# Value projections by seven block products, the convolution's norm by halves beside them, key copies spread over the steps

## The chip, the cores and the metric

The kernel is one program on one core of a Trainium2 chip. The metric is the device time of one execution in microseconds (us). The median of three runs before the change is 1679.09 us. A core has a matrix engine (TensorE, PE in the profile), a vector engine (VectorE, DVE), a scalar engine (ScalarE, ACT), GpSimd (POOL) and SyncE (SP), whose queue issues nearly all transfers here. Each engine works through its own list of instructions in order and waits on semaphores for the others.

## The reference

One block on 1024 tokens with 1024 channels, float32 throughout:

```
h = rms_norm(x, g_pre_mix)
z = h @ w_in            # q, k, v (3 groups x 8 heads x 64 each), glu_in (2048), z_ga, z_gc (1024 each)
y_attn = dilated_attention_mixer(q, k, v)          # groups (window, dilation): (128,1) (512,4) (2048,16)
y_conv = conformer_conv_mixer(glu_in)              # GLU, depthwise conv of 31 taps, layer_norm, silu, @ w_conv_out
merged = sigmoid(z_ga) * y_attn + sigmoid(z_gc) * y_conv
x = x + rms_norm(merged @ w_mix_out, g_post_mix)
x = x + rms_norm(swiglu_ffn(rms_norm(x, g_pre_ffn), w_ffn_in, w_ffn_out), g_post_ffn)
```

Within the attention each of the three groups gives an output and a log of its softmax denominator for each head; the three outputs of a head slot are added with the softmax of these logs as weights, and the sum (512 wide) goes through `w_attn_out`. The layer norm of the convolution is taken over the channels, for each token.

## The kernel before, in words

**Products.** Every float32 operand is split into two fp32r parts, `hi` (a rounded copy, ScalarE, L214) and `lo` (what is left, a subtraction on POOL or VectorE, L215); a product is hi·hi + hi·lo + lo·hi, three matmuls. Most projections are written by `winograd`: two weights' blocks and two token halves with seven block products in place of eight, from sums of weight blocks (`quarters`) and sums of token blocks T1 to T4 (`quarter_sums`). The six value jobs (`v`, two halves of the heads for each of three groups) are plain instead. For each of 8 tiles of 128 tokens and each of 8 channel blocks there is one matmul over 512 columns (L1137, the tokens' hi against the weights' hi and lo side by side) and one over 256 (L1138, the tokens' lo against the weights' hi). ScalarE copies the bank and POOL adds its two halves (L1159).

**The stages.** With channels on partitions, the gates, the convolution's input and the queries and keys are projected first (span 0 to 543.7 us), while VectorE works on the depthwise convolution. Then come the six value jobs, one late gate (`plain_gate`), sixteen convolution-out units (`unit`, L336 to L338, each 8 blocks x 3 matmuls over 512 tokens, closed on VectorE by L1947), sixteen attention-out units of half the length, the mix projection (L2025) and the feed-forward layers (L352 to L354, L2281).

**What runs beside them.** Order is set by counting. Each `tick` of a product hands on background work: steps put off with `later(k, ...)` run k ticks on, and generators given to `bg` go on after as many ticks as they yield. `conv_norm`, the layer norm of the convolution, is such a generator: it starts with the means over channels (L1499, two matmuls with a column of 1/1024 against `csum`, which the end of the convolution fills), then subtracts, squares, sums, takes the reciprocal root (`rstd`) and applies gain and silu, over 1024 tokens at a time. Eight blocks of the convolution come back from memory for it.

The attention is a generator too, moved on by `beat`: each call adds `RATE` to a credit and each whole credit is one small step (RV = 0.42 beside value products, RU = 0.8 beside units). It has 12 stacks (3 groups x 4 pairs of heads) of 8 steps u, so 96 steps, in a pipeline: `att_s` the scores (L1258, L1262), `att_e` the exponentials, `att_t` transposes (L1301, copies L1308 and L1309), `att_p` the products with the values (L1335), `att_o` the outputs. A stack needs its keys twice, with the other head's rows zeroed; `double` makes that tile on POOL (L1076 to L1078), for both heads at once, at u == 7 of the stack before and at u == 2 of its own. `stack_load` fetches queries, keys and values.

**The merge.** For each of the four head pairs `merge` waits until the attention has ended, and then multiplies, adds and splits the three groups' outputs on VectorE: L1438, L1442, L1447, L1452 (each 128 x 1024), L1457 (a sum with a change of order), a copy on ScalarE (L214) and L215. The results are the operands `OT` of the attention-out units; the block kt of such a unit needs the merge of pair kt. What a merge has not yet issued when the convolution-out units are over is issued there in one go (`B.finish`).

**Loads around the units.** The second convolution-out weights are loaded 14 ticks into the late gate, the first gate tile (`d_gc`) 1 tick after it. The first three units take the first token half of three output blocks, the next three the second; after that the halves alternate.

Of the kernel before, what the change touches and what calls it, by code (L numbers as in the profile page):

```python
# [15 lines left out]
T = 1024  # L16
D = 1024
KT = 8
H = 512
# [29 lines left out]
NSLOT = 42  # L49

# [14 lines left out]
class Build:  # L65
# [236 lines left out]
    def pair(self, i):  # L302
# [12 lines left out]
        if n < len(J) and J[n][2] == "row1":  # L315
# [5 lines left out]
            self.queued = n + 2  # L321
        elif n < len(J):
            todo += [(3, lambda: self.load_ahead(n + 1)), (16, lambda: self.queue_split(n + 1))]
# [139 lines left out]
    def rstd(self, acc, n, eps_col, gap=3):  # L463
# [3 lines left out]
        ps = self.bank("s")  # L467
# [13 lines left out]
        for b in range(0, nt, 4):  # L481
            pb = self.bank("s")
# [587 lines left out]
    def double(self, p, hf):  # L1070
# [3 lines left out]
        z = ops["z"][hf] = self.slot(F32R)  # L1074
        for h in range(2):
# [88 lines left out]

    LT, LP = 4, 5
# [4 lines left out]
    def attention(self):  # L1170
# [12 lines left out]
        while s < total + self.LP:  # L1183
            if s < total:
# [33 lines left out]
                for _ in range(1 + (u == 1 and not order)):  # L1218
                    if nxt and nxt[5] < 5:
                        self.stack_load(nxt)  # L1220
# [263 lines left out]
    def conv_norm(self):  # L1484
        nc = self.nc
        mean = self.slot()
        A = []

        def load():
            A.append(self.slot())  # L1490
            nc.sync.dma_start(A[-1], self.d_conv[len(A) - 1])

        for _ in range(4):
            load()
        yield 3
        for hf in range(2):
            s = slice(hf * H, (hf + 1) * H)
            ps = self.bank("s")
            nc.tensor.matmul(ps, self.mean_col.to_broadcast([128, 128]), self.csum[:, s], start=True, stop=True)  # L1499
            nc.scalar.copy(mean[:, s], ps)  # L1500
        self.csum = None
        yield 1
        q = []
        for b in range(10):
            if b < 4:
                load()
            if b < 8:
                nc.vector.tensor_tensor(A[b], A[b], mean, op=OP.subtract)
            if 0 < b < 9:
                q.append(self.slot())  # L1510
                nc.scalar.activation(q[-1], A[b - 1], AF.Square)
            if b > 2:
                p = q.pop(0)
                nc.vector.tensor_tensor(q[0], q[0], p, op=OP.add)
            p = None
            yield 3 - b % 2
        mean = None
        yield 3
        pb = yield from self.rstd(q[0], T, self.eps_ln, 6)
        rs = self.slot()  # L1520
        for hf in range(2):
# [875 lines left out]
```

## Time and profile before

| what | value |
|---|---|
| runs | 1680.42, 1679.09, 1678.84 us (median 1679.09) |
| profiled execution, its own time | 1681.52 us |
| its span | 1679.7 us |
| TensorE busy | 1661.0 us (99%), 8027 matmuls |
| VectorE, ScalarE, POOL busy | 1272.0, 828.0, 543.2 us |
| mean granted TensorE clock | 0.998 |
| transfers | 289.64 MB, mean 172 GB/s |
| value jobs end, convolution-out units end (span) | 771.6, 905.8 us |

"Span" is the time from the first to the last recorded instruction; the execution's own time is a little longer. The busy time of an engine is the sum of its instructions' durations, and a group's row gives busy time, mean ns of one, idle time before it and what ended that idleness. A line number (L1137) is the line of the kernel that issued the instruction. PEclk and "clock" are the TensorE clock that was granted, as a share of full speed.

### The profile page before, as it was taken

How to read it: one execution, taken by the hardware profiler on the slowest of the kernel's cores; microseconds unless marked ns; L12 is line 12 of the kernel's file. 1: busy time of each engine (PE TensorE's matmuls, PEld its weight loads, DVE VectorE, ACT ScalarE, POOL GpSimd, SP SyncE). 2: the span in 40 equal slices, each digit the busy share in tenths (PEclk: the TensorE clock that was granted, in tenths of full speed). 3: DMA queues.
4: the chain of work that ended last, by engine and by line, in shares of the span. 5: the costliest groups of instructions: out<-in, count | busy, mean ns of one | idle time of the engine just before them, and what ended most of it. 6: DMA issues, size and time to landing. Idle time of an engine off the chain costs nothing.

```text
span 1679.7 us, 23382 instructions
## 1 busy us (share of the span) xinstructions
PE 1661.0 (99%) x8027; PEld 1386.2 (83%) x8027; DVE 1272.0 (76%) x2268; ACT 828.0 (49%) x1646; POOL 543.2 (32%) x456
## 2 busy tenths in 40 slices
PE   9999999999999999999899999999999999999998
PEld 7788888888888888988788888888888888888886
DVE  7998988789999767778885746877655566576686
ACT  7454443434444578888722447633333333354453
POOL 0038777887876356867300300000000000000000
PEclk9999999999999999999999999999999999999999
DMA  4435433455566887879998524134132223494334
GB/s 181 155 101 187 139 132 133 152 185 176 188 166 172 282 269 215 256 228 251 296 300 294 188 88 164 63 132 150 73 128 95 94 94 111 167 372 127 114 118 156
DMA packets 165178, 289.64 MB, mean 172 GB/s; under 512 B 47689, under 2 KB 79812, under 8 KB 165060
## 3 DMA queue, kind: packets, MB, share of 16 engines
q1 hardware_dynamic: 164420, 287.45, 52.8%
q8 instruction: 63, 1.03, 0.2%
q14 instruction: 55, 0.45, 0.1%
q10 hardware_dynamic: 288, 0.52, 0.1%
q0 software_dynamic: 352, 0.18, 0.1%
HBM read 197.39 MB, written 95.42 MB: 174 GB/s over the span
## 4 chain that ended last, share of the span: by engine, by line
PE 85%; issue 5%; POOL 3%; DMA 3%; DVE 2%; ACT 2%; SPq 0%; DVEq 0%; POOLq 0%; ACTq 0%
PE p L354 16%; PE p L353 16%; PE p L352 16%; PE p L2281 12%; PE p L2025 5%; PE p L1137 4%; PE p L336 2%; PE p L337 2%; PE p L338 2%; PE p L1138 2%; PE p L655 2%; PE p L1335 1%; DMA datt<-d 1%; PE p L1301 1%; PE p L1262 1%
## 5 line engine op out<-in xcount | busy, mean ns | idle before, releaser
L352 PE MATMUL p<-b,b 128*128 128x512 f32 x1316 | 512.6, 390 | 0.0
L354 PE MATMUL p<-b,b 128*128 128x512 f32 x1316 | 512.4, 389 | 0.3
L353 PE MATMUL p<-b,b 128*128 128x512 f32 x1316 | 512.1, 389 | 0.1
L354 PEld LDWEIGHTS p<-b,b 128*128 128x128 f32 x1316 | 247.0, 188 | 52.7 <-POOL b L215 1.5
L352 PEld LDWEIGHTS p<-b,b 128*128 128x128 f32 x1316 | 247.0, 188 | 52.5 <-ACT c L411 0.5
L353 PEld LDWEIGHTS p<-b,b 128*128 128x128 f32 x1316 | 247.0, 188 | 51.7 <-DVE b L1473 0.5
L2281 PE MATMUL p<-b,b 128*128 128x512 f32 x924 | 209.6, 389 | 0.0
L2281 PEld LDWEIGHTS p<-b,b 128*128 128x128 f32 x924 | 173.4, 188 | 36.0
L868 DVE SCALAR_TENSOR_TENSOR p<-b,par,p 128x511 f32<-128x511 f32 (+14 forms) x232 | 163.5, 738 | 0.0
L1137 PE MATMUL p<-b,b 128*128 128x512 f32 x384 | 144.3, 408 | 0.1
L214 ACT CAST b<-d 128x1024 fp32r<-128x1024 f32 x82 | 86.1, 1050 | 100.6 <-POOL d L237 56.5
L215 POOL TENSOR_TENSOR b<-d,b 128x1024 fp32r<-128x1024 f32 x43 | 104.1, 2422 | 47.6 <-ACT b L214 39.0
L1473 DVE TENSOR_TENSOR b<-b,b 128x512 fp32r<-128x512 f32 x141 | 98.4, 704 | 17.9 <-ACT b L1472 16.3
L1138 PE MATMUL p<-b,b 128*128 128x256 f32 x384 | 107.9, 281 | 0.0
L215 DVE TENSOR_TENSOR b<-d,b 128x1024 fp32r<-128x1024 f32 x39 | 47.6, 1221 | 79.0 <-ACT b L214 79.0
L1472 ACT CAST b<-b 128x512 fp32r<-128x512 f32 x141 | 86.5, 619 | 41.4 <-PE p L2281 17.8
L214 ACT CAST b<-b 128x1024 fp32r<-128x1024 f32 x51 | 53.6, 1052 | 89.2 <-POOL b L246 38.8
L336 PE MATMUL p<-b,b 128*128 128x512 f32 x240 | 96.2, 401 | 0.0
L1276 ACT ACTIVATE c<-c,stat 128x128 f32<-128x128 f32 (+1 forms) x192 | 85.1, 447 | 18.8 <-DVE stat L1266 17.4
L337 PE MATMUL p<-b,b 128*128 128x512 f32 x240 | 93.6, 390 | 0.0
L338 PE MATMUL p<-b,b 128*128 128x512 f32 x240 | 93.6, 390 | 0.0
L2025 PE MATMUL p<-b,b 128*128 128x512 f32 x384 | 89.9, 392 | 0.0
(248 smaller groups left out, 2899.4 us busy)
## 6 DMA issues: line engine op xcount, KB each, us to landing
b<-w_in SPq DMA_DIRECT2D x33, 512.0 KB, 5.6
b<-w_fi SPq DMA_DIRECT2D x29, 512.0 KB, 4.3
d<-w_in SPq DMA_DIRECT2D x25, 512.0 KB, 4.5
dk<-c SPq DMA_DIRECT2D x48, 256.0 KB, 4.1
dq<-c SPq DMA_DIRECT2D x48, 256.0 KB, 3.6
b<-dk SPq DMA_DIRECT2D x48, 256.0 KB, 6.8
d<-w_fi SPq DMA_DIRECT2D x22, 512.0 KB, 3.6
dqS<-c SPq DMA_DIRECT2D x44, 256.0 KB, 2.1
```

Source lines behind the costliest of these rows:

```text
L214: self.nc.scalar.copy(hi, x)
L215: self.wsplit.tensor_tensor(lo, x, f(hi), op=OP.subtract)
L336: nc.tensor.matmul(ps, hi[:, s], a, start=kt == 0, stop=False)
L337: nc.tensor.matmul(ps, hi[:, s], b, start=False, stop=False)
L352: nc.tensor.matmul(ps, hi[:, s], a, start=first and kt == 0, stop=False, skip_group_check=True)
L353: nc.tensor.matmul(ps, hi[:, s], b, start=False, stop=False, skip_group_check=True)
L354: nc.tensor.matmul(ps, lo[:, s], a, start=False, stop=kt == 3, skip_group_check=True)
L868: nc.vector.scalar_tensor_tensor(A[i][:, j:], src[i][:, :H - j], w[i], A[i][:, j:], op0=OP.mult, op1=OP.add)
L1137: nc.tensor.matmul(ps, a, w, start=kt == 0, stop=kt == KT - 1, skip_group_check=True)
L1138: nc.tensor.matmul(ps[:, 256:], b, w[:, :256], start=False, stop=kt == KT - 1, skip_group_check=True)
L2025: nc.tensor.matmul(banks[tt][nh], st, wt[:, nh * H:(nh + 1) * H], start=bool(kt == 0 and a), stop=bool(kt == KT - 1 and b))
L2281: nc.tensor.matmul(acc[t], x, y, start=first and e == 0, stop=last and e == 2, skip_group_check=True)
```

## The change

Four of the six value jobs (`QUADS = 2`, two jobs each) leave `v` for a new function `quad`. It computes two jobs by seven block products, from sums of weight blocks (S1 to S4, A11, A12, A22) and the token sums T1 to T4 that the earlier projections used. The tokens' sums stand still as the matmul's stationary 128 x 128 operand; the weights' blocks move, 256 columns at a time. Each product is 4 channel blocks x 4 token tiles x 3 matmuls (`quad_prod`, L1216, L1218, L1219). The weights' sums are made on VectorE, their split is a copy on ScalarE and a subtraction on POOL (L1199).

The convolution's norm now works on one token half at a time and runs beside the quads; its means (L1645) are asked for when it is given to the background. The attention starts after the quads: its first loads 30 ticks into the second quad, its steps with the first of the two value jobs that are left. `double` makes one head's copies per call, at u == 6, 7, 8 and 1. The second convolution-out weights are loaded at tick 6 of the late gate, the first gate tile at tick 9 of it. Two output blocks, not three, start with their first half.

```diff
+QUADS = 2
...
     def double(self, p, hf, heads=(0, 1)):
...
-        for h in range(2):
+        for h in heads:
             nc.gpsimd.memset(f(z[parts[1 - h], h * H:(h + 1) * H]), 0.0)
             nc.gpsimd.tensor_copy(z[parts[h], h * H:(h + 1) * H], f(ops["k"][h][parts[0], s]))
             nc.gpsimd.tensor_copy(ops["c"][h][parts[1], s], f(ops["q"][parts[h], s]))
...
+    def quad_prod(self, ps, w, rhs, first):
+        hi, lo = w
+        for kt in range(4):
+            a, b = rhs[kt]
+            n = slice(kt * 256, (kt + 1) * 256)
+            for c in range(4):
+                o = ps[c // 2][:, c % 2 * 256:(c % 2 + 1) * 256]
+                t = slice(c * 128, (c + 1) * 128)
+                nc.tensor.matmul(o, a[:, t], hi[:, n], start=first and kt == 0 and c % 2 == 0, stop=False, ...)
+                nc.tensor.matmul(o, a[:, t], lo[:, n], ...)
+                nc.tensor.matmul(o, b[:, t], hi[:, n], ...)
+                if c % 2:
+                    self.tick()
...
+    def quad(self, q, T, then):
+        for k, step in ((1, lambda: self.quad_split(q, "A12")), (2, lambda: self.quad_sum(q, "S1")),
+                        (3, lambda: self.quad_sum(q, "S3")), (4, lambda: self.quad_sum(q, "S2")),
+                        (7, lambda: self.quad_sum(q, "S4")), (8, lambda: self.quad_split(q, "S2")),
+                        (13, lambda: self.quad_split(q, "S1")), (21, lambda: self.quad_split(q, "S3")),
+                        (29, lambda: self.quad_split(q, "S4")), (37, lambda: self.quad_split(q, "A22"))):
+            self.later(k, step)
...
+        X, Z = two(), two()
+        self.quad_prod(X, w.pop("A11"), operands("B11"), True)
+        x1 = copy(X, ja)
+        self.quad_prod(Z, w.pop("A12"), operands("B21"), True)
+        add(Z, x1, ja, 0)
+        self.quad_prod(X, w.pop("S2"), operands("T2"), False)
+        x2 = copy(X, ja)
+        V = two()
+        self.quad_prod(V, w.pop("S1"), operands("T1"), True)
+        v1 = copy(V, jb)
+        self.quad_prod(X, w.pop("S3"), operands("T3"), False)
+        add(X, v1, jb, 1)
+        self.quad_prod(V, w.pop("S4"), operands("B22"), False)
+        add(V, x2, ja, 1)
+        self.quad_prod(X, w.pop("A22"), operands("T4"), False)
...
-                if u == 7 and nxt:
-                    self.double(nxt, 0)
-                if u == 2:
-                    self.double(cur, 1)
+                if u in (6, 7) and nxt:
+                    self.double(nxt, 0, (u - 6,))
+                if u == 8 and nxt:
+                    self.double(nxt, 1, (0,))
+                if u == 1:
+                    self.double(cur, 1, (1,) if cur[2]["z"][1] else (0, 1))
...
     def conv_norm(self):
+        means = [average(0), average(1)]
+        self.csum = None
+        for j in range(4):
+            self.later((0, 0, 5, 10)[j] + 1, lambda j=j: load(0, j))
+        yield 5
         for hf in range(2):
...
-            B.later(14, lambda: B.load_ahead(co[1]))
+            B.later(6, lambda: B.load_ahead(co[1]))
+            B.later(9, lambda: first_gate.append(gate_load(B.d_gc[0])))
...
+    for i, q in enumerate(B.quads):
+        if i == QUADS - 1:
...
+            B.later(30, lambda: next(att))
...
+        B.quad(q, B.T, B.quads[i + 1] if i + 1 < QUADS else None)
...
+    B.fine = att
     for i, (g, hg) in enumerate(vj):
         B.v(g, hg, vs[i], vs[i + 1])
-        if i == 0:
-            next(att)
-            B.fine = att
...
-    for n, hf in [(n, hf) for hf in range(2) for n in range(3)] + [(n, hf) for n in range(3, 8) for hf in range(2)]:
+    for n, hf in [(n, hf) for hf in range(2) for n in range(2)] + [(n, hf) for n in range(2, 8) for hf in range(2)]:
```

In the rows below p is a bank of PSUM, b a tile in SBUF, d a scratch tile, c an attention tile; a tile's own number is the last one.

TensorE at the start of the value stage. Before, twenty rows of the first value job (L1137, L1138) stand ahead of the two means of the convolution's norm (L1499); these are the last four of them, the means, and what follows:

```order
L1137 MATMUL p728_4913<-b706_4800,b73_631 128x512
L1138 MATMUL p728_4913<-b706_4800,b73_631 128x256
L1137 MATMUL p728_4913<-b706_4800,b76_642 128x512
L1138 MATMUL p728_4913<-b706_4800,b76_642 128x256
L1499 MATMUL p729_4922<-b232_1635,mean_col_282 128x512
L1499 MATMUL p730_4925<-b232_1635,mean_col_282 128x512
L1137 MATMUL p728_4913<-b707_4820,b77_652 128x512
L1138 MATMUL p728_4913<-b707_4820,b77_652 128x256
```

After, six rows of the first quad's first product stand ahead of the means (L1645); these are the last three of them:

```order
L1216 MATMUL p717_4870<-b708_4818,b73_631 128x256
L1218 MATMUL p717_4870<-b709_4819,b73_631 128x256
L1219 MATMUL p717_4870<-b708_4818,b73_631 128x256
L1645 MATMUL p723_4886<-b232_1635,mean_col_282 128x512
L1645 MATMUL p725_4890<-b232_1635,mean_col_282 128x512
L1216 MATMUL p718_4871<-b708_4818,b73_631 128x256
L1218 MATMUL p718_4871<-b709_4819,b73_631 128x256
L1219 MATMUL p718_4871<-b708_4818,b73_631 128x256
```

So the means have moved from behind ten pairs of products to behind six narrow ones.

POOL where the attention starts. Before, sums of value products (L1159) stand between the key copies of the first stack's two halves (`double`, L1076 to L1078):

```order
L1077 CAST b776_5233<-b757_5111 64x512
L1078 CAST b759_5116<-b755_5106 64x512
L1159 TENSOR_TENSOR d783_5295<-b719_4879 128x512 x2
L1159 TENSOR_TENSOR d793_5405<-b719_4879 128x512 x2
L1076 MEMSET b803_5482 64x512
L1077 CAST b803_5482<-b756_5108 64x512
L1078 CAST b758_5114<-b755_5106 64x512
```

After, the last weight splits of the quads (L1199) are followed by the copies (L1083 to L1085) of both heads of the first half and then of both heads of the second, twelve rows in one piece, of which the first three are shown:

```order
L1199 TENSOR_TENSOR b807_5667<-b764_5246,b806_5666 128x1024
L1199 TENSOR_TENSOR b823_5758<-d766_5292,b822_5757 128x1024
L1083 MEMSET b826_5849 64x512
L1084 CAST b826_5849<-b810_5679 64x512
L1085 CAST b812_5685<-b809_5677 64x512
```

So no sum of value products stands any more between the copies that the first stack needs.

VectorE at the end of the merges. Before, the last row of the last merge (L215) has four ends of units (L1947) behind it, the first two of which follow here:

```order
L1947 SCALAR_TENSOR_TENSOR b1656_9289<-p1670_9375,par_306,b1656_9289 128x512
L1452 TENSOR_TENSOR d1606_8996<-d1606_8996,b1672_9385 128x1024
L1947 SCALAR_TENSOR_TENSOR b1656_9289<-p1677_9419,par_306,b1656_9289 128x512
L197 TENSOR_TENSOR b1682_9459<-b1668_9371,b1681_9458 128x512
L1457 TENSOR_TENSOR b1683_9465<-b1663_9320,d1606_8996 128x8x128
L197 TENSOR_TENSOR b1682_9459<-b1668_9371,b1681_9458 128x512
L215 TENSOR_TENSOR b1685_9479<-b1683_9465,b1684_9478 128x1024
L1947 SCALAR_TENSOR_TENSOR b1669_9373<-p1680_9451,par_306,b1669_9373 128x512
L1947 SCALAR_TENSOR_TENSOR b1669_9373<-p1686_9490,par_306,b1669_9373 128x512
```

After, the end of the last unit is the first row (L2108), and the last two rows of the third merge (L1604, L217) and the whole fourth merge (L1585 to L1604, L217) follow it, ahead of the first attention-out unit's end (L2134):

```order
L2108 SCALAR_TENSOR_TENSOR b1673_9623<-p1700_9770,par_306,b1673_9623 128x512
L1604 TENSOR_TENSOR b1702_9802<-b1676_9635,d1575_9155 128x8x128
L217 TENSOR_TENSOR b1704_9805<-b1702_9802,b1703_9804 128x1024
L1585 TENSOR_TENSOR b1697_9747<-b1697_9747,b1698_9757 128x1024
L1589 TENSOR_TENSOR b1699_9766<-b1699_9766,b1701_9778 128x1024
L1594 TENSOR_TENSOR b1697_9747<-b1697_9747,b1699_9766 128x1024
L1599 TENSOR_TENSOR d1635_9409<-d1635_9409,b1705_9809 128x1024
L1604 TENSOR_TENSOR b1706_9815<-b1697_9747,d1635_9409 128x8x128
L217 TENSOR_TENSOR b1708_9818<-b1706_9815,b1707_9817 128x1024
L199 TENSOR_TENSOR b1714_9832<-b1688_9714,b1713_9831 128x256
L2134 TENSOR_TENSOR b1689_9716<-p1712_9827,b1689_9716 128x512
```

So eight rows of merging now stand behind the end of the last unit, where none stood. In all, the attention's 96 steps stood 73 beside value products and 23 beside six units; they now stand 44 beside two value jobs and 52 beside twelve units.

More of the change, by code (lines that the diff above doesn't have):

```diff
@@ L321, in pair @@
             self.queued = n + 2
+        elif n < len(J) and J[n][2] == "values":
+            self.quad_first(self.quads[0], (2, 9, 11, 13, 19))
         elif n < len(J):
@@ L466, in rstd @@
         nt = n // 128
-        ps = self.bank("s")
+        tag = "s" if "s" in self.tags else "g"
+        ps = self.bank(tag)
         for t in range(nt):
@@ L481, in rstd @@
         for b in range(0, nt, 4):
-            pb = self.bank("s")
+            pb = self.bank(tag)
             for t in range(b, min(nt, b + 4)):
@@ new lines, in quad_prod @@
+    def quad_prod(self, ps, w, rhs, first):
+        nc = self.nc
+        hi, lo = w
[5 more added lines that the diff above has]
+                t = slice(c * 128, (c + 1) * 128)
+                nc.tensor.matmul(o, a[:, t], hi[:, n], start=first and kt == 0 and c % 2 == 0, stop=False,
+                                 skip_group_check=True)
+                nc.tensor.matmul(o, a[:, t], lo[:, n], start=False, stop=False, skip_group_check=True)
+                nc.tensor.matmul(o, b[:, t], hi[:, n], start=False, stop=kt == 3 and c % 2 == 1, skip_group_check=True)
+                if c % 2:
+                    self.tick()
@@ L1217, in attention @@
                         nxt = self.stacks(*order.pop(0))
-                for _ in range(1 + (u == 1 and not order)):
+                for _ in range(1 if order else 3):
                     if nxt and nxt[5] < 5:
@@ L1485, in conv_norm @@
         nc = self.nc
[L1486 to L1495, printed above, removed]
-        for hf in range(2):
[L1497 to L1516, printed above, removed]
@@ L1534, in conv_norm, with load, average @@
-        nc.scalar.activation(rs[:, :1], self.eps_ln, AF.Exp)
-        rs = None
-        yield 11
+        add = nc.vector.tensor_tensor
+        A = {}
+        def load(hf, j):
+            x = self.slot()
+            for e in range(2):
+                b = 2 * j + e
+                nc.sync.dma_start(x[:, e * H:(e + 1) * H], self.d_conv[b][:, hf * H:(hf + 1) * H])
+                A[hf, b] = x[:, e * H:(e + 1) * H]
+        def average(hf):
+            ps = self.bank()
+            nc.tensor.matmul(ps, self.mean_col.to_broadcast([128, 128]), self.csum[:, hf * H:(hf + 1) * H],
+                             start=True, stop=True)
+            m = self.half()
+            nc.scalar.copy(m, ps)
+            return m
@@ L1888, in build @@
     assert bl not in B.gens
-    B.banks(g=2, s=2, t=2, o=2)
-    B.bank("s")
     B.OT, B.merges = {}, []
```

180 lines of the change are left out of this document (144 added, 36 removed).

## The prediction

> **What bounds the kernel now.** I read the page first: TensorE is busy for 99% of the span.
>
> ```profile
> span 1679.7 us, 23382 instructions
> PE 1661.0 (99%) x8027; PEld 1386.2 (83%) x8027; DVE 1272.0 (76%) x2268; ACT 828.0 (49%) x1646; POOL 543.2 (32%) x456
> PE 85%; issue 5%; POOL 3%; DMA 3%; DVE 2%; ACT 2%; SPq 0%; DVEq 0%; POOLq 0%; ACTq 0%
> ```
>
> So time is won where matmul columns disappear, and lost wherever TensorE is made to wait. Next I cut the span into stages (table of windows): value jobs with the convolution's norm, value jobs with attention, attention beside the convolution-out units, those units alone, and the attention-out units. The columns are the busy times (and counts), granted clock, DMA share and GB/s.
>
> ```profile
> 543.70:612.00 68.30, 66.60 (x382) 57.37 (x382) 48.01 (x57) 44.27 (x69) 25.28 (x23) 1.00 0.87 283
> 612.00:771.60 159.60, 157.19 (x1160) 144.17 (x1161) 123.77 (x424) 133.31 (x417) 118.05 (x162) 0.99 0.82 235
> 771.60:842.00 70.40, 64.74 (x415) 54.74 (x415) 59.73 (x190) 55.23 (x172) 33.31 (x46) 1.00 1.02 283
> 842.00:905.80 63.80, 63.80 (x284) 52.69 (x283) 45.73 (x51) 14.15 (x24) 3.60 (x6) 1.00 0.93 292
> ```
>
> TensorE idles 1.7, 2.4 and 5.7 us in the first three and not at all in the fourth: that fourth stretch is 64 us of plain units, and under it VectorE finishes the attention (`merge`). Remember it; the change takes half of it away.
>
> **The products.** The start times of matmuls give their price (timeline); a record's own duration includes the pipeline.
>
> ```profile
> 560.30 0.39 PE L1137 MATMUL p<-b,b 128*128 128x512 f32 x1
> 560.53 0.28 PE L1138 MATMUL p<-b,b 128*128 128x256 f32 x1
> ...
> 574.86 0.39 PE L1137 MATMUL p<-b,b 128*128 128x512 f32 x1
> ...
> 618.23 0.39 PE L1262 MATMUL p<-b,b 128*128 128x256 f32 x2
> 618.46 0.60 PE L1301 MATMUL p<-ident,c 128*128 128x128 f32 x4
> ```
>
> A value job is 64 pairs of a 512- and a 256-wide product. From 560.30 to 574.86 there are 42 pairs: 0.347 us each. Four jobs less remove 4 x 64 x 0.347 = 88.8 us. Two `quad` calls add 2 x 7 x 48 = 672 products, all 256 wide. Two such (L1262, attention's scores), each with weights of its own, take 0.23 us to the start of the next instruction: 0.115 us each, 77.3 us in all. Gain 11.5 us. Inside a pair the 256-wide product takes 0.347 - 0.23 = 0.117 us; by that it is 78.6 us and the gain 10.2. I take the row in which narrow products follow each other, as they will in a quad: -11.5.
>
> The quads' other work lies beside them. A product of a quad lasts 48 x 0.115 = 5.5 us and needs one pair of weights, a copy on ScalarE and a subtraction on POOL:
>
> ```profile
> L214 ACT CAST b<-d 128x1024 fp32r<-128x1024 f32 x82 | 86.1, 1050 | 100.6 <-POOL d L237 56.5
> L215 POOL TENSOR_TENSOR b<-d,b 128x1024 fp32r<-128x1024 f32 x43 | 104.1, 2422 | 47.6 <-ACT b L214 39.0
> ```
>
> That is 1.05 + 2.42 us, issued at least 7 ticks (4.8 us) ahead; POOL has 7 x 2.42 = 17 us of it in the 39 us of a quad. The reads of PSUM between products have a whole other product as cover, since X, Z and V take turns. The convolution's norm keeps its operations, in halves of half the length. I cost all this at nothing; were a subtraction late at every second product, by some 0.6 us, it would be 4 us, the bound.
>
> **The norm's means, moved ahead.** As the rows of TensorE show, ten pairs of value products stood ahead of the two matmuls that sum `csum`; now six narrow ones do. What the means wait for is the end of the convolution:
>
> ```profile
> 541.30 1.08 DVE L1019 TENSOR_TENSOR c<-p,c 128x512 f32<-128x512 f32 x1
> 543.54 0.68 DVE L208 TENSOR_TENSOR b<-b,b 128x512 fp32r<-128x512 f32 x1
> 544.14 0.68 DVE L881 TENSOR_TENSOR b<-p,c 128x512 f32<-128x512 f32 x1
> 544.97 2.70 POOL L893 TENSOR_TENSOR b<-b,b 128x1024 f32<-128x1024 f32 x1 [10.32 <-DVE b L881]
> 547.73 0.70 PE L1499 MATMUL p<-b,mean_col 128*128 128x512 f32 x1 [0.25 <-POOL b L893]
> ```
>
> POOL's sum ends at 547.7. L1019 reads a product's bank in both kernels and so stays where it is; of the value weights' splits on VectorE (L208) one falls away behind it, so the sum ends some 0.6 us sooner, at 547.1. TensorE starts the stage at 543.7 and, with 0.1 us for the switch and 0.7 us of products, stands at the means at 544.5: a wait of 2.6 us where it was 0.25, so +2.4. All that is queued behind them on TensorE waits too; the other engines have work of their own and only get ahead.
>
> **The clock.** A short wait can cost more than itself (table of windows, and the waits around it):
>
> ```profile
> 609.73:613.14 3.41, 1.96 (x11) 1.43 (x10) 1.91 (x10) 3.41 (x12) 3.20 (x5) 1.00 1.05 389
> 613.14:616.56 3.42, 3.42 (x15) 3.13 (x14) 1.90 (x9) 1.82 (x7) 3.20 (x5) 0.50 1.04 215
> PE p L1258 <- POOL b L1077: 1.3, 1, 1.3
> ```
>
> After a stretch of 3.41 us with 1.96 us of work the granted clock was 0.50 for the next 3.42 us, which costs about 1.7 us. The wait for the means could do the same: +0.9 as half of it, bounds 0 and 1.7. The Trainium skill (TensorE: Matmul & The Clock Gate, "What's actually happening") says the clock halves after at least one idle window of about 3.4 us; by that rule a wait of 2.6 us would not halve it and this term would be 0. The row above disagrees, since there 1.5 us of idleness was enough.
>
> **The start of attention.** That wait of 1.3 us was for POOL. As POOL's rows show, the second pair of key copies stood behind a sum of value products (L1159), which waits for TensorE itself; now all four pairs stand together behind the last weight split of the quads, with nothing ahead of them that waits for a value job. I take the wait (1.3 us, and 0.2 us behind it) and its slow clock (1.7) as gone: -3.2, bounds 0 and -3.2.
>
> **Attention, twice as long beside the units.** Attention has 96 steps. Before, 73 stand among value products and 23 among six units; now 44 among two value jobs and 52 among twelve units. Its own matmuls are the same. The 5.7 us of idleness in 771.6 to 842 include two waits on a ScalarE or VectorE that stood for a late load:
>
> ```profile
> 802.95 0.38 PE L1335 MATMUL p<-c,b 128*128 128x256 f32 x1 [1.49 <-ACT c L1308]
> 814.16 0.44 PE L1335 MATMUL p<-c,b 128*128 128x128 f32 x2 [1.37 <-ACT c L1308]
> ACT b L196 <- DMA b<-w_co: 1.5, 1, 1.5
> DVE b L1947 <- DMA b<-dgc: 2.0, 1, 2.0
> ```
>
> The change issues both loads (the second convolution-out weights, the first gate) 8 ticks sooner: -2.9, or nothing if they are late all the same. The other 2.8 us double with the steps: +2.8. But DMA is full there (share 1.02), and a stack's keys, queries and values must come through beside twelve units now: +1.5, bounds 0 and +12.
>
> **The tail.** `merge` starts its VectorE work when attention has ended, and the attention-out units need all four merges. VectorE's rows show it: before, four units' ends follow the last merge; now the end of the third merge and all of the fourth stand behind the end of the last unit, and before the first attention-out unit. The prices (groups of VectorE and ScalarE from 841 to 893, and the first and the last row of the merges in the timeline):
>
> ```profile
> L1947 DVE SCALAR_TENSOR_TENSOR b<-p,par,b 128x512 f32<-128x512 f32 x9 | 6.7, 742 | 4.0 <-PE p L338 4.0
> L1438 DVE TENSOR_TENSOR b<-b,b 128x1024 f32<-128x1024 f32 x4 | 5.0, 1248 | 0.0
> L215 DVE TENSOR_TENSOR b<-b,b 128x1024 fp32r<-128x1024 f32 x4 | 4.9, 1232 | 0.7 <-ACT b L214 0.7
> L1447 DVE TENSOR_TENSOR b<-b,b 128x1024 f32<-128x1024 f32 x4 | 4.9, 1232 | 0.0
> L1457 DVE TENSOR_TENSOR b<-b,d 128x1024 f32<-128x1024 f32 x2 | 4.2, 2123 | 0.0
> ...
> L214 ACT CAST b<-b 128x1024 fp32r<-128x1024 f32 x4 | 4.2, 1054 | 25.4 <-DVE b L1457 25.4
> ...
> 841.98 1.23 DVE L1438 TENSOR_TENSOR b<-b,b 128x1024 f32<-128x1024 f32 x1
> ...
> 891.54 1.23 DVE L215 TENSOR_TENSOR b<-b,b 128x1024 fp32r<-128x1024 f32 x1 [0.66 <-ACT b L214]
> ```
>
> In the new order: 0.75 (the unit's end), 2.1 (L1457's successor), 1.05 on ScalarE, 1.2 for the rest of the third merge; then four times 1.2, 2.1, 1.05 on ScalarE and 1.2. That is 14.3 us, some 14.8 with the hand-overs between engines. TensorE has 9 products of the next unit that need no fourth merge, 2 us: a stall of 12.6 us. The same from the other side: the merges took from 841.98 to 892.8, 51 us; now six units are left to cover them, 6 x 24 x 0.225 = 32 us (284 products in 63.8 us), which lacks 19 us at the old pace. Bounds 10 (hand-overs cheaper, the first products longer) and 19; I take the chain, 12.6, since its ticks are dropped at the end of the units. An idle stretch of that length halves the clock again, for one window or two: +1.8, bounds 1.7 and 3.4.
>
> **The sum.** -11.5 + 2.4 + 0.9 - 3.2 - 2.9 + 2.8 + 1.5 + 12.6 + 1.8 = +4.4 us. The profiled execution took 1681.5 us (its span 1679.7), 2.4 above the median of the runs, 1679.1; on the median that is 1683.5, and I say 1684.
>
> **Rivals.** One, on the faster side: the tail is covered. If VectorE and the loads run far enough ahead that less than 6.6 us of stall is left, the time is over 0.2% below; at none, 1683.5 - 14.4 = 1669. For it: VectorE is busy 72% from 842 to 905.8, so there is room. Against it: its queue is in order and the rows stand behind the last unit's. Two: transfers starve attention beside the units. 283 GB/s at share 1.02 say that nothing is free there; 12 us more give 1695. Against: only 2.9 of 5.7 us idle were seen behind loads. Three: the narrow products are bound by their weight loads, recorded at 0.188 us each:
>
> ```profile
> L2281 PEld LDWEIGHTS p<-b,b 128*128 128x128 f32 x924 | 173.4, 188 | 36.0
> ```
>
> 672 x 0.188 = 126 us, 49 more, 1733. Against it the pair of L1262 at 0.115.
>
> **Chances.** Forecast (tail paid, 1676 to 1690) 0.62, of which 0.02 faster, 0.25 same, 0.35 slower; tail covered 0.16 (0.15 faster, 0.01 same); starved transfers 0.20; weight loads 0.02. A measurement tells 0.2%, 3.4 us, from no change. Together 0.17 faster, 0.26 same, 0.57 slower. The range 1673 to 1696 leaves out half of the second case, a fifth of the third and the fourth.
>
> **What would show it.** Right: 672 starts 0.115 us apart; L1645 waiting 2 to 3 us for POOL; no wait of attention's first steps on POOL; behind the last L2108 TensorE idle for some 8 us on ScalarE's copy of the fourth merge, with a granted clock of 0.50 after it. Wrong: TensorE without a gap between the last convolution-out unit and the first attention-out unit, or many new waits of L1482 on loads.

## The result, and the profile after

The changed kernel is slower: 1702.24 us in the median (1697.33 to 1706.53, 5 runs) against 1679.09 before, a ratio of 1.0134 with a 95% interval of 1.0118 to 1.0149. The forecast was 1684, with 1696 as its upper end: the sign was right, the size was not. The execution that was profiled took 1697.33 us (span 1695.5), 15.8 more than the one profiled before; it is the fastest of its five, so a second trace of the same kernel (a0_again, 1704.0 us, 22.5 more) is used beside it.

The page of the first trace, in its head, its chain of waits and one group:

```profile
span 1695.5 us, 23828 instructions
PE 1658.0 (98%) x8187; PEld 1391.9 (82%) x8187; DVE 1289.5 (76%) x2300; ACT 833.0 (49%) x1647; POOL 558.4 (33%) x454
PE 57%; DVE 3%; DMA 2%; ACT 1%; issue 1%; DVEq 0%; SPq 0%; ACTq 0%
L340 PE MATMUL p<-b,b 128*128 128x512 f32 x240 | 99.5, 415 | 9.2 <-ACT b L216 9.2
```

TensorE has 3.0 us less work recorded in a span that is 15.8 us longer. Where the longer time lies, the table of windows tells by stage: the quads, the two plain value jobs with attention, attention beside the units, units alone, the tail. After a stretch and its length stand the busy times (and counts) of TensorE, its weight loads, VectorE, ScalarE and POOL, then the granted clock, the DMA share and GB/s.

```profile
543.80:640.10 96.30, 89.30 (x701) 86.31 (x699) 66.96 (x83) 54.96 (x78) 45.78 (x28) 0.96 0.65 205
640.10:736.50 96.40, 92.68 (x688) 85.20 (x688) 73.48 (x251) 79.73 (x249) 67.03 (x92) 1.00 0.85 243
736.50:874.00 137.50, 130.66 (x863) 114.18 (x862) 115.51 (x378) 105.90 (x336) 75.85 (x108) 0.99 0.94 273
874.00:908.60 34.60, 34.60 (x154) 28.42 (x154) 29.89 (x37) 9.70 (x17) 2.71 (x5) 1.00 0.90 276
908.60:928.00 19.40, 9.00 (x24) 5.85 (x24) 13.83 (x12) 3.32 (x5) 1.14 (x1) 0.65 1.03 371
```

TensorE idles 7.0, 3.7, 6.8, 0 and 10.4 us in them. In the tail the forecast chain is there: the last unit ends, and VectorE (first rows) and ScalarE (last two) work through the end of the third merge and all of the fourth, while TensorE waits.

```profile
907.78 0.75 DVE L2108 SCALAR_TENSOR_TENSOR b<-p,par,b 128x512 f32<-128x512 f32 x1 [3.57 <-PE p L342]
908.44 2.01 DVE L1604 TENSOR_TENSOR b<-b,d 128x1024 f32<-128x1024 f32 x1
911.57 1.23 DVE L217 TENSOR_TENSOR b<-b,b 128x1024 fp32r<-128x1024 f32 x1 [1.11 <-ACT b L216]
...
917.50 2.00 DVE L1604 TENSOR_TENSOR b<-b,d 128x1024 f32<-128x1024 f32 x1
920.66 1.23 DVE L217 TENSOR_TENSOR b<-b,b 128x1024 fp32r<-128x1024 f32 x1 [1.17 <-ACT b L216]
910.49 1.04 ACT L216 CAST b<-b 128x1024 fp32r<-128x1024 f32 x1 [11.61 <-DVE b L1604]
919.59 1.04 ACT L216 CAST b<-b 128x1024 fp32r<-128x1024 f32 x1 [8.05 <-DVE b L1604]
```

Busy time hides part of a loss, because a record's duration includes the pipeline and a slow clock stretches it. So the table below counts lost time by the starts of the matmuls: for each, the time to the next start, less what it takes where nothing waits (0.227 us for 512 columns, 0.117 for 256, 0.058 for 128, 0.110 for a transpose), differences below zero counted as none, added up by stage. The first column goes to the attention's first score product. By these prices the change's products are 9.4 us less work. Attention beside values lasts 164 us before the change and 95 to 98 after it.

| kernel, time of the traced execution | stage's start to attention | attention beside values | attention beside units | tail |
|---|---|---|---|---|
| before, 1681.5 | 3.7 | 22.6 | 14.9 | 0 |
| changed, 1697.3 | 15.4 | 12.9 | 24.0 | 14.2 |
| changed, second trace, 1704.0 | 19.0 | 15.6 | 22.9 | 14.2 |
| e4 before, attention late, 1702.4 | 4.7 | 13.2 | 26.2 | 18.3 |
| e1 merges early, 1713.3 | 19.6 | 13.3 | 33.7 | 15.0 |
| e6 RU = 1.0, 1697.9 | 18.9 | 15.5 | 31.8 | 0.5 |
| e5 no norm arithmetic, 1689.1 | 11.5 | 10.6 | 23.1 | 14.9 |
| f1 no norm at all, 1685.9 | 7.4 | 9.9 | 24.2 | 14.0 |
| g1 splits on VectorE, 1716.6 | 25.2 | 16.8 | 24.0 | 18.1 |
| e7 one quad, 1682.2 | 7.2 | 13.4 | 16.1 | 10.1 |
| q1 one quad, RU = 0.9, 1677.9 | 8.8 | 13.5 | 18.7 | 0 |
| q2 the same, RV = 0.46, 1683.1 | 7.2 | 15.3 | 24.8 | 0 |

The sums close: the second trace loses 32.1 us more than before in the whole span (1.7 of it ahead of these stages), less 9.4 of products is 22.7, and the execution took 22.5 more.

### The profile page after: what moved, and what is told of

It reads as the page before. It is cut to its first block, busy times and chain, and to the rows that moved or that the text cites. A ratio compares the mean times of both kernels' runs of the same rounds, so it can differ in the third digit from the quotient of the medians.

```text
span 1695.5 us, 23828 instructions
## 1 busy us (share of the span) xinstructions
PE 1658.0 (98%) x8187; PEld 1391.9 (82%) x8187; DVE 1289.5 (76%) x2300; ACT 833.0 (49%) x1647; POOL 558.4 (33%) x454
## 4 chain that ended last, share of the span: by engine, by line
PE 57%; DVE 3%; DMA 2%; ACT 1%; issue 1%; DVEq 0%; SPq 0%; ACTq 0%
PE p L2442 12%; PE p L357 8%; PE p L356 8%; PE p L358 8%; PE p L2186 5%; PE p L340 2%; PE p L341 2%; PE p L342 2%; PE p L1482 2%; PE p L1144 2%; PE p L1448 1%; PE p L1409 1%; PE p L1145 1%; PE p L1405 1%; DMA b<-dq 1%
## 5 line engine op out<-in xcount | busy, mean ns | idle before, releaser
L356 PE MATMUL p<-b,b 128*128 128x512 f32 x1316 | 512.7, 390 | 0.0
L358 PE MATMUL p<-b,b 128*128 128x512 f32 x1316 | 512.4, 389 | 0.2
L357 PE MATMUL p<-b,b 128*128 128x512 f32 x1316 | 512.1, 389 | 0.1
L358 PEld LDWEIGHTS p<-b,b 128*128 128x128 f32 x1316 | 247.0, 188 | 53.2 <-POOL b L217 1.5
L356 PEld LDWEIGHTS p<-b,b 128*128 128x128 f32 x1316 | 247.0, 188 | 52.3 <-ACT c L415 0.5
L357 PEld LDWEIGHTS p<-b,b 128*128 128x128 f32 x1316 | 247.0, 188 | 51.6 <-DVE b L1620 0.5
L2442 PE MATMUL p<-b,b 128*128 128x512 f32 x924 | 209.6, 389 | 0.0
L2442 PEld LDWEIGHTS p<-b,b 128*128 128x128 f32 x924 | 173.4, 188 | 36.0
L217 POOL TENSOR_TENSOR b<-d,b 128x1024 fp32r<-128x1024 f32 x43 | 104.1, 2422 | 47.6 <-ACT b L216 39.0
L1620 DVE TENSOR_TENSOR b<-b,b 128x512 fp32r<-128x512 f32 x141 | 100.5, 719 | 15.5 <-ACT b L1619 13.8
L340 PE MATMUL p<-b,b 128*128 128x512 f32 x240 | 99.5, 415 | 9.2 <-ACT b L216 9.2
L217 DVE TENSOR_TENSOR b<-d,b 128x1024 fp32r<-128x1024 f32 x39 | 47.6, 1221 | 79.3 <-ACT b L216 79.3
L341 PE MATMUL p<-b,b 128*128 128x512 f32 x240 | 95.4, 398 | 1.2 <-DVE b L217 1.2
L342 PE MATMUL p<-b,b 128*128 128x512 f32 x240 | 95.1, 396 | 0.0
L2186 PE MATMUL p<-b,b 128*128 128x512 f32 x384 | 90.0, 392 | 0.0
L217 POOL TENSOR_TENSOR b<-b,b 128x1024 fp32r<-128x1024 f32 x24 | 57.7, 2404 | 86.6 <-ACT b L216 86.6
L2186 PEld LDWEIGHTS p<-b,b 128*128 128x128 f32 x384 | 71.4, 188 | 14.4
```

What stands on the lines that cost most here:

```text
L217: self.wsplit.tensor_tensor(lo, x, f(hi), op=OP.subtract)
L340: nc.tensor.matmul(ps, hi[:, s], a, start=kt == 0, stop=False)
L341: nc.tensor.matmul(ps, hi[:, s], b, start=False, stop=False)
L342: nc.tensor.matmul(ps, lo[:, s], a, start=False, stop=kt == nk - 1)
L356: nc.tensor.matmul(ps, hi[:, s], a, start=first and kt == 0, stop=False, skip_group_check=True)
L357: nc.tensor.matmul(ps, hi[:, s], b, start=False, stop=False, skip_group_check=True)
```

## The experiments

**The kernel again** (a0_again). No edit.

> The changed kernel once more, unaltered, as the base of the others. Its five runs lay between 1697.3 and 1706.5 us, and the profile (1697.3) is of the fastest of them. Theory: what varies are waits behind transfers, at the start of attention and beside the convolution-out units, since transfers are at full share there (1.01 to 1.04); a median of 1699 to 1705 and, in the trace, the same tail of some 14 us behind the last convolution-out unit and the same 0.120 us for a narrow product. Rival: the runs differ in the clock that follows the tail's idleness; then the tail itself differs between this trace and the first by several us.

1701.12 us (1700.53 to 1704.0). The tail is 14.2 us again. What differs most is the quads: a longer wait for the norm (L474, the reciprocal root's sums), 3.6 us where the first trace has 1.0. VectorE's wait for a load (the last row) is as long in the first trace, 5.6 us. The waits of TensorE, and that one of VectorE (us in total, times, the longest):

```profile
PE p L340 <- ACT b L216: 9.9, 2, 7.3
PE p L1482 <- DVE c L1456: 7.2, 7, 3.3
PE p L474 <- DVE c L1667: 3.6, 1, 3.6
PE p L1218 <- POOL b L1199: 2.6, 1, 2.6
PE p L1645 <- POOL b L898: 2.5, 1, 2.5
DVE b L1661 <- DMA b<-dconv: 5.5, 1, 5.5
```

So the rival is out for these two traces, which differ by waits ahead of the tail. Of the theory's two places only the stretch beside the values loses more (2.7 us); beside the units it is 1.1 less.

**Lateness alone** (e4), on the kernel before:

```diff
+        if i == 3:
+            B.later(6, lambda: next(att))
         B.v(g, hg, vs[i], vs[i + 1])
-        if i == 0:
-            next(att)
+        if i == 3:
             B.fine = att
-    ... for hf in range(2) for n in range(3)] + [(n, hf) for n in range(3, 8) ...
+    ... for hf in range(2) for n in range(2)] + [(n, hf) for n in range(2, 8) ...
```

(The generator also gets a pause before its first step.)

> The kernel before, with all six value jobs plain, but the attention begins only with the last two of them (its first loads 6 ticks into the fourth), and two output blocks rather than three start with their first half, as in the changed kernel. Nothing is changed in the products or the norm. Theory (the attention's lateness is the larger loss: by TensorE's starts, value jobs, units and tail lost some 53 us in the second trace of the changed kernel and some 35 before): 14 to 20 us more than before, 1693 to 1699, with a tail of over 8 us behind the last unit. Rival (the quads' own waits and the full transfers around them are the loss, and lateness costs only the tail's VectorE chain, part of which the idler value jobs win back): under 6 us more.

1699.76 us (1693.91 to 1702.4), ratio 1.0121 [1.0100, 1.0142]: about as much as the change loses, with no quad in the kernel. The attention beside values loses 8.4 us less (with what stands ahead of it), beside units 11.3 more, and the tail is 18.3. TensorE's largest wait from 734 us on is the merges' copy:

```profile
PE p L336 <- ACT b L214: 13.0, 2, 10.4
PE p L1336 <- DVE c L1310: 3.1, 5, 1.0
```

So a late start of the attention makes the kernel slower by itself. How much of the change's own loss it is, the table tells: the last three columns of the changed kernel come to 13.6 and 15.2 us more than before (20.2 in e4, which lacks the spread copies and the early loads), and the quads' stage loses 11.7 and 15.3 more for 9.4 us of products saved. What the quads save they lose themselves, with 2.3 to 5.9 us on top, and the late start is the larger part.

**The tail, by merging sooner** (e1). The first two pairs may start at step 80; pauses of 7, 9 and 4 ticks become 3, 2 and 2.

```diff
-        while not self.ending or hp > self.turn:
+        while not (self.soon if hp < 2 else self.ending) or hp > self.turn:
...
-        yield 7
+        yield 7 if hp < 2 else 3
-        while self.fine is not None or hp > self.done:
+        while hp > self.done:
```

> The merges of the first two head pairs may start 16 steps ahead of the attention's end, and the merges' pauses are shorter, so that of all merging only the last split stands behind the end of the last convolution-out unit; nothing else changes. Theory (the tail is paid in full, 14.2 us of lost products and slow clock): 11 to 14 us less than the changed kernel, about 1690, with no gap over 2 us before the first attention-out unit. Rival (VectorE, 84% busy beside the units, has no room): the merges push the attention's own VectorE work back, the same time is lost between 820 and 905 us, and the total stays within 3 us of 1702.

1713.31 us: worse by 11, and both theories missed. 10.8 us more than in the second trace are lost beside the units, as the rival had it, but the tail did not go either. It has another cause: the load of the softmax weights (`dw`), asked for in a stretch that is full of transfers, came late. That the shorter pauses made it so is read from the trace and was not tried apart. TensorE's wait:

```profile
PE p L340 <- ACT b L216: 12.0, 1, 12.0
```

VectorE's row in the timeline:

```profile
928.45 1.23 DVE L1590 TENSOR_TENSOR b<-b,b 128x1024 f32<-128x1024 f32 x1 [7.64 <-DMA b<-dw]
```

**The tail, by a faster attention** (e6). `RV, RU = 0.42, 1.0`.

> The changed kernel with RU = 1.0 in place of 0.8: more of the attention's steps for each unit, so that the last scores stand ten unit ends ahead of the first attention-out unit where eight stood; all but the last split of the merges is now ahead of the last unit's end. Theory (the tail is set by the lead of the attention's end over the units' end): the tail falls from 14 us to under 6, of which 3 to 6 us come back as waits beside the units, 3 to 8 us less in all. Rival (transfers: they are at full share from 900 us on, and with the merges earlier their broadcast loads are later than VectorE): the gap ahead of the second attention-out product stays over 8 us, only behind a load, and the time is within 3 us of 1702, or above.

1696.22 us, some 5 less in the median, though the intervals of the ratios overlap (1.0091 to 1.0125, and 1.0110 to 1.0144 for the kernel again). The tail is 0.5 us: it does hang on the lead of the attention's end. But 8.9 of the 13.7 us come back beside the units (first row; the second is the tail). VectorE is busy for 84% there, no more than in the changed kernel, so its share does not explain it; the cause is not shown.

```profile
742.00:875.00 133.00, 122.95 (x807) 106.06 (x806) 111.63 (x373) 104.27 (x336) 74.34 (x108) 0.97 0.92 268
921.10:926.00 4.90, 4.72 (x21) 3.56 (x20) 3.38 (x5) 1.36 (x3) 0.73 (x1) 1.00 1.03 411
```

**The quads: the wait for the means** (e2).

```diff
+        yield 3
         means = [average(0), average(1)]
...
-        yield 5
+        yield 2
```

> The two means of the convolution's norm are asked for 3 ticks later on TensorE, behind 30 narrow products where 6 stood ahead of them; what follows them keeps its ticks. Theory (the wait of 2.5 us and the half clock behind it cost 5.3 us by the first trace's starts, where 2.2 were lost before the change): 3 to 5 us less than the changed kernel, no wait of the means on POOL, granted clock 1.00 at 545 to 552 us. Rival (the idle time only moves, because the norm's later steps are then late for the quads): within 1.5 us of it.

1705.53 us, not less. The means' wait for POOL is gone, but the quads lose 16.0 and the tail 16.4. TensorE now waits for the norm's later sums, 5.8 us where the two traces of the changed kernel have 1.0 and 3.6:

```profile
PE p L474 <- DVE c L1668: 5.8, 2, 3.8
```

The theory of 3 to 5 us fell; the idle time only moved, as the rival had it, though the time came out 3 to 4 us higher, outside its 1.5.

**The quads: the second half's loads** (e3), `self.later(1, ...)` in place of `self.later(8, ...)` for `load(1, ...)`.

> The loads of the convolution's second token half are put off by 1 tick in place of 8, so that they stand ahead of the first half's stores on SP's queue. Theory (VectorE stood 5.6 us at its first subtraction for such a load, the sums of the second quad's weights stood behind it, then POOL's split, then TensorE for 2.7 us at 598 us): that wait goes, 2.5 to 4 us less. Rival (the second quad's weights are late on their own, since their loads wait for a free tile until 581 us): the wait at 598 us stays and the time is within 1 us of the changed kernel's.

1705.46 us, not less; the quads lose 22.6. The waits move to the weights:

```profile
PE p L1218 <- POOL b L1199: 4.1, 2, 2.1
PE p L1216 <- ACT b L1196: 2.1, 2, 1.1
PE p L474 <- DVE c L1667: 1.2, 1, 1.2
DVE d L1180 <- DMA d<-w_v: 6.7, 1, 6.7
```

The last row is VectorE's: the load of value weights, for which it does not wait in the first trace, now comes 6.7 us late, while its wait for the convolution's load falls from 5.6 to 1.6 us. An earlier load makes another one late, as the rival said in part; whether it is the queue or the transfers was not separated.

**The quads without the norm's arithmetic (e5), and without the norm (f1).** In the first the subtractions, squares, sums, `rstd` and activations are left out; in the second the loads and stores too, and `conv_split` reads `d_conv`.

> The changed kernel with the arithmetic of the convolution's norm left out (VectorE's and ScalarE's operations, the reciprocal root); its two means, its loads and its stores stay, in their ticks. Theory (the norm, squeezed from 159 us into the 96 us of the quads, stands ahead of the weights' sums on VectorE and makes TensorE wait for it: 2.8 us at 599, 3.8 at 615 and the slow clock behind them): the quads take 86 to 90 us where they took 96 to 100, and the time falls by 7 to 12 us. Rival (the quads' loads are late because transfers are full): the quads still wait for POOL's splits and the time falls by less than 4 us.

> The changed kernel with the convolution's norm left out but for its two means: no arithmetic, no loads, no stores; the convolution-out units read the convolution itself. With the arithmetic alone left out the quads lost 11.5 us to waits and slow clock where they lost 19.0 with it. Theory (the rest is the norm's 8 MB of transfers, with the tiles they hold: the second quad's first weights waited 7.8 us on SP's queue and its split held TensorE at 598): the quads lose 5 to 7 us, what the means and their slow clock cost, and the time is 1683 to 1688. Rival (the rest is the quads' own: their seven weight splits on ScalarE and POOL and their copies of banks): still 9 us or more lost, 1689 to 1693.

1691.61 and 1685.11 us. The quads lose 11.5 and 7.4 us where the second trace lost 19.0 and the first 15.4: 3.9 to 7.5 us are the norm's arithmetic and 4.1 its transfers and tiles. Both times are as their theories had them; e5's quads (90.7 us) and f1's lost time (7.4) end just above theirs. e5 leaves out more than waits: the root's 24 small products on TensorE (2.7 us at their spacing) go too, of which 0.9 us counts as lost by the table's prices, before the change as well. Without the arithmetic the waits of L474 are gone, and one wait for a weight split is left:

```profile
PE p L1218 <- POOL b L1199: 2.4, 1, 2.4
```

Without the norm's transfers that one is gone too. Most of what is left in the quads are 2.0 us of products that take 0.120 and not 0.117 us, the wait of 2.5 us for the means, and the clock behind it.

**The splits on VectorE** (g1, g2), `nc.vector.tensor_tensor(lo, ...)` in `quad_split`, with two quads and with one.

> The changed kernel with the fourteen subtractions of the quads' weight splits on VectorE instead of POOL. In the second trace a subtraction of the norm that meets such a split on POOL lasts 2.88 us where its neighbours last 0.68, and it ends when POOL does. Theory (what crowds VectorE in the quads is POOL holding it, not the number of its operations): VectorE does each split in 1.2 us and loses no 2.2 us to POOL, the wait at 599 for POOL and the 3.6 us for the norm's sums go, and the quads lose 11 to 14 us where they lost 19: 1694 to 1698. Rival (VectorE's own queue and the late loads are it, and 17 us more work for it makes them worse): 19 us or more lost, 1701 to 1706.

> The same edit with one quad and RU = 0.9 (1677.6 us with the splits on POOL). Theory (POOL holding VectorE delays the norm, and so the attention's start): the norm ends 3 to 5 us sooner, 1673 to 1676. Rival (with one quad the norm is held by its loads, and the attention by transfers): within 1.5 us of 1677.6.

1713.79 and 1681.85 us: the theory fell, the rivals were too mild. VectorE's queue now stands for seven of the fourteen splits, from 540 to 660 us (g1):

```profile
DVE b L1199 <- ACT b L1196: 18.4, 6, 7.3
DVE b L1199 <- PE p L1218: 6.3, 1, 6.3
```

A split waits for ScalarE's copy, and that, in three cases (11.5 us), for a product of TensorE. On POOL nothing of the norm stands behind a split; on VectorE all its subtractions and sums do. This points to the queue's order more than to POOL's hold on VectorE.

**One quad** (`QUADS = 1`; e7), and with other rates (q1, q2).

> The changed kernel with one quad (two value jobs by seven products) and four plain value jobs; the norm may then go on beside the first plain job, and the attention begins when it has ended. Theory (each quad saves 4 us of products; what costs is the crowding of the norm and the late attention): the attention begins some 10 to 15 us later than before, not 35, the tail is under 7 us, 1685 to 1694. Rival (the norm waits for VectorE all the same, since the splits of value weights are there as well): over 1697.

> One quad and RU = 0.9 in place of 0.8, so that the attention ends sooner; all else as in the run with one quad (1683.2 us, tail 10.1, attention beside the units 16.1 us lost). Theory (as with two quads: tail paid by the late attention, and a faster one buys it with waits): the tail falls to 1 to 4 us, 2 to 4 us more are lost beside the units, 1676 to 1680 in all. Rival (beside the units the engines are full and each step sooner costs as much as it saves, as RU = 1.0 gave back 8.9 of 13.7 us): 1681 to 1684.

> One quad, RU = 0.9 and also RV = 0.46 in place of 0.42, so that beside the three or four plain value jobs left the attention is faster too. Theory (beside value products TensorE lost 13.4 us in 109 with one quad, 20 in 160 before, so there is a little room there): the attention ends 6 to 9 us sooner than with one quad and the old rates, the tail is under 2 us, 1674 to 1678. Rival (VectorE and ScalarE set the attention's pace already, and a higher rate only makes TensorE wait in its queue): the end of the attention stays within 3 us of the one with RU = 0.9 alone and the time is not lower.

1683.18, 1677.57 and 1683.13 us. With one quad the last scores come 20 to 26 us sooner than in the changed kernel's two traces and the tail is 10.1, more than expected, though the time is below the 1685 to 1694 of the theory; RU = 0.9 takes it away for 2.6 us of waits beside units. RV = 0.46 wins nothing: the end of the attention stays within 0.3 us and the waits beside the units grow from 18.7 to 24.8, as its rival said. q1 is 0.9988 [0.9978, 0.9997] of the time before.

> One quad, RU = 0.9, and the means of the convolution's norm asked for 3 ticks later. In the run with one quad and RU = 0.9 (1677.6 us) the wait for the means and the half clock behind it lost some 5 us by TensorE's starts. Theory (with one quad the norm has time enough, so that what the means don't lose isn't given back): 3 to 5 us less, 1672.5 to 1675. Rival (as with two quads, where the same edit gained nothing, what is won at the start is lost to transfers or to the norm's later steps): 1676 to 1679.

(f2, on q1.) 1679.67 us (1673.88 to 1685.65): nothing won, and wider spread. The trace shows a wait that q1 does not have, for a load of queries between 700 and 900 us:

```profile
PE p L1409 <- DMA b<-dq: 3.4, 3, 1.6
```

**Two parts of the change on the kernel before**: `double` by heads (p1), and then also the two loads 8 ticks sooner (p2).

> The kernel before with one part of the change alone: the key copies one head at a time, at u = 6, 7, 8 and 1 of a stack. Theory (POOL's copies held TensorE only at the attention's first steps, 1.3 us and its slow clock, where the second pair is now asked for one step sooner but still behind the sums of value products): 0 to 3 us less than before, 1676 to 1679. Rival (POOL is not the limit of attention, and copies asked for sooner only collide with the value parts): within 1 us of before, either way.

> The kernel before with two parts of the change: the spread copies, and the second convolution-out weights and the first gate tile loaded 8 ticks sooner. Theory (the waits of 1.5 and 2.0 us for these two loads stood behind TensorE's waits at 801 and 813 us, and they are gone in every trace with the early loads): 2 to 5 us less than before, 1674 to 1677. Rival (transfers are at full share there, so an earlier load makes another one late): within 1 us of the run with the copies alone.

1677.98 us, ratio 0.9983 [0.9974, 0.9993], and 1675.79 us, 0.9973 [0.9963, 0.9983]. The intervals overlap, so the loads' own share isn't settled; in the traces the two kernels lose the same, and with the copies alone only 0.3 us of the two loads' waits beside the attention is left. Against the first theory, the wait of 1.3 us at the attention's start is still there in both traces; what went are waits later, among value products (22.6 to 19.2 lost) and beside the units (14.9 to 12.0). The second of these kernels has the lowest median of all that were run, and beats both the kernel before and the changed one; it holds none of the quads.

## Why the prediction was wrong in size

The forecast was +4.4 us; the two traces took 15.8 and 22.5 us more than the one before. By the table, first trace and second: the products -9.4, the stage up to the attention +11.7 and +15.3, attention beside values -9.7 and -7.0, beside units +9.1 and +8.0, the tail +14.2, and +1.7 ahead of these stages in the second.

- **Products: -11.5; measured -8.2.** The starts of the narrow products are 0.120 us apart, nine of them here:

```profile
554.79 0.28 PE L1218 MATMUL p<-b,b 128*128 128x256 f32 x1
...
555.87 0.28 PE L1218 MATMUL p<-b,b 128*128 128x256 f32 x1
```

  672 x 0.120 = 80.6 us, from 88.8. The pair of L1262 that the price was taken from (0.115) was the wrong one (the 88 products of that shape in the same trace have a median spacing of 0.119); the 256-wide product inside a value pair, 0.117 and named as the other bound, was nearer.
- **The means: +2.4 and +0.9; right in place and size of the wait, 2.5 us.** The granted clock was then 0.50 from 547.2 to 550.6 (rows in the last section), so the clock's term is at its upper bound, 1.7. With 2.3 for the wait (2.5 less the 0.25 of before) the two are 4.0, where 3.3 was forecast.
- **The quads' other work, costed at nothing with 4 us as the bound: the step that failed.** The stage loses 11.7 and 15.3 us more than before, where the means were to cost 3.3. Some 2 us of the rest are the narrow products' price, counted above; 6 to 10 us are left for a term that stood at nothing. The runs without parts of the norm put 11.6 of the second trace's 19.0 us (8.0 of the first's 15.4) down to the norm. The prediction costed it as "its operations, in halves of half the length". It left out that the norm's products stand in TensorE's own queue and hold it until VectorE has made their sums: 3.6 us at L474 in the second trace, with the clock at 0.50 for 6.8 us behind it,

```profile
617.90:624.70 6.80, 5.86 (x27) 5.89 (x28) 1.58 (x6) 2.72 (x4) 2.37 (x1) 0.50 0.87 243
```

  and both are gone in e5, which has neither these sums nor these products. It also left out that the norm's loads and their tiles compete with the second quad's weights: the wait of 2.6 us for a split goes only in f1. Whether the transfers or the tiles cause that one stays open.
- **The start of attention: -3.2.** The wait on POOL went, as foretold. Another came in its place, 3.2 to 3.3 us at the first outputs (L1482 for VectorE's L1456), whose buffer a store of values (`dv<-c`, put off by `later(6, ...)`) was still reading:

```profile
657.37 0.69 DVE L1456 TENSOR_TENSOR c<-p,c 128x512 fp32r<-128x512 f32 x1 [4.71 <-DMA dv<-c]
```

  That this store's lateness is the cause is read from the trace and was not tried.
- **Attention beside the units: -2.9 + 2.8 + 1.5; measured +8 to +9.** The two late loads are gone from the waits, as foretold; that issuing them sooner did it isn't shown, since p1 has hardly any of these waits without it. The doubling was done on 5.7 us of idle time; by starts the same stretch lost 14.9. The second error is one of method: idle time was read as lost time. It hardly moved the total, by luck: the steps that left the value jobs took their losses with them, so that both attention stages together come to -0.6 and +1.0 us, where -1.8 was forecast (-3.2 and +1.4).
- **The tail: +12.6 + 1.8; measured 14.2.** Right in place and mechanism; the sum is right because two misses cancel. TensorE idled 10.4 us, not 12.6 (the waits for ScalarE's copies were 2.6 and 6.6 to 7.3), and the slow clock cost the other 3.8, above its bound of 3.4, at 0.50 until the new units are under way:

```profile
910.70:914.10 3.40, 1.72 (x3) 0.69 (x3) 2.53 (x3) 0.83 (x1) 0.00 (x0) 0.76 1.02 246
914.10:917.50 3.40, 0.00 (x0) 0.00 (x0) 3.33 (x4) 0.00 (x0) 0.00 (x0) 0.50 1.02 360
917.50:920.90 3.40, 0.22 (x1) 0.22 (x1) 2.23 (x2) 1.31 (x3) 0.00 (x0) 0.50 1.03 407
920.90:924.30 3.40, 2.93 (x7) 1.95 (x8) 2.92 (x4) 0.35 (x2) 1.14 (x1) 0.50 1.04 420
```

- **The rivals.** The tail was not covered. Starved transfers did not come as forecast: beside the units L1482 waits for VectorE's L1456, and that for ScalarE (16.7 us in 22 waits, first trace), not for loads. But three of the four edits that put TensorE or a load ahead found a later transfer in the way (e1, e3, f2; in e2 it was the norm's sums). The weight loads did not bind: 0.120 us from start to start, not 0.188.

## What to carry to other kernels

Before a saving of matmul columns is counted, ask what the saved stage was hiding: here 8 us of products were bought by starting the attention over 30 us later, and that alone cost 21 us in e4. Count a stage's loss by the spacing of matmul starts, not by idle time, when it is to be scaled to a longer stage. And where several engines' queues are nearly full, an edit that removes one wait is worth nothing until a run shows that no other takes its place.

## What was not expected of the hardware

TensorE waited 2.5 us for the means and was granted half the clock right after it (table of windows, first trace of the changed kernel):

```profile
547.20:548.60 1.40, 1.36 (x2) 0.84 (x3) 1.36 (x2) 0.00 (x0) 1.40 (x1) 0.50 1.14 313
548.60:550.60 2.00, 2.00 (x4) 0.67 (x2) 2.00 (x1) 0.59 (x1) 1.87 (x1) 0.50 1.21 276
```

The Trainium skill (TensorE: Matmul & The Clock Gate, "What's actually happening") asks for at least one idle window of about 3.4 us; the trace disagrees here too, with 2.5. A wait of this length does not always do it: behind the one of 2.6 us at 599 us in the second trace the clock stayed at 1.00.

A VectorE operation on two SBUF tiles that starts beside a subtraction on POOL ends only behind it, at 611.30 us against 610.76, and lasts 2.88 us where its neighbours take 0.68 (second trace):

```profile
608.03 2.73 POOL L1199 TENSOR_TENSOR b<-d,b 128x1024 fp32r<-128x1024 f32 x1 [3.62 <-PE p L1219]
607.82 0.68 DVE L1661 TENSOR_TENSOR b<-b,c 128x512 f32<-128x512 f32 x1
608.42 2.88 DVE L1667 TENSOR_TENSOR c<-c,c 128x512 f32<-128x512 f32 x1
```

In the two traces of the changed kernel fourteen of the fifteen such operations over 512 columns that start beside a split on POOL, over 0.1 us ahead of its end, end 0.55 us after it; the six with one operand in PSUM (L1264, L1266) keep their 0.68 us there.

The Trainium skill (Trainium Architecture — The Big Picture, "What this means for kernel authors") calls the port that these two share an exclusive lock; the trace agrees, and the runs with the splits on VectorE, which were slower, suggest that the order of a queue can still weigh more.
